# One core, an encoder layer: the list scheduler of the w_o stage gets a landing time for each kind of transfer, and three first evictions go through ScalarE

## The chip, the cores and the metric

The kernel runs on one core of a Trainium2 chip. The metric is the device time of one execution in microseconds; the time of a kernel is the median of its runs. The profile is one more execution of the same program, with its own time.

## The reference, cut to what matters

The reference is one layer of an encoder over 1024 tokens of 1024 channels, in float32. Two branches (a gated mixing of positions and a windowed attention) are merged with sigmoid gates; the merged tensor is multiplied by `w_o`, scaled by a per-channel gate and added to the input; the sum is normalised and goes through a feed-forward network (FFN). The change lies in the middle line of these:

```
merged = jax.nn.sigmoid(gate_a) * a_out + jax.nn.sigmoid(gate_b) * b_out
x = x + gt1 * (merged @ w_o)

h2 = rmsnorm(x, norm2_g) * (1.0 + sc2) + sh2
f_gate, f_up = jnp.split(h2 @ w_ffn_in, 2, axis=-1)
x = x + gt2 * ((jax.nn.silu(f_gate) * f_up) @ w_ffn_out)
```

## The kernel before, in words

Channels lie on the partitions and tokens along the free axis, so the 1024x1024 activations are eight tiles of 128 channels for each half of 512 tokens. A float32 product is made from three passes over operands that are split into a high part (a cast, on ScalarE) and a low part (source minus high part, on VectorE). The large products use a scheme with seven block products in place of eight. Most instructions are issued through one helper, so nearly all rows of the profile have the line L145 (in the changed file L143) and are told apart by their tiles.

`out_products` is the stage of `w_o`. It works on four pairs p0 to p3 of output tiles, and for each pair it makes seven block products, named in the table `USE`: M1, M2, T2, T3, T4, T1 and B22. A product is 12 matmuls of 128x512 (4 blocks by 3 passes). TensorE runs them in three lists: `first` holds the eight products M1 and M2, `second` the twelve T2, T3, T4, and `third` the eight T1, B22. For a pair, M1, T2, T3 and T4 accumulate in the same PSUM bank ("a", tile `mm`). After each of them VectorE reads the bank (an eviction: bank times a gate column, added to a row tile), and the next product of that pair may write the bank only after this eviction has read it. M2 goes to a bank of its own ("b", tile `at`), T1 and B22 share bank "c".

The operands: the token blocks are sums of parts of `merged`, split into high and low tiles. `T1` is tile `tt1h/tt1l`, `T2` is `tt2h/tt2l`, `B22` is `b22h/b22l`; `T3` and `T4` are plain `mid` tiles, made in `blocks` by `negsum` (a SCALAR_TENSOR_TENSOR mid<-mid,mid), a cast and a subtraction (TENSOR_TENSOR mid<-mid,mid). The weights come as units of 1024 columns, loaded into the tile `raw` (three buffers), cast to `wh` and completed with `wl` (three buffers each). `need` asks for them: kind "0" and "B" are parts of `w_o`, kinds "A" and "C" are sums that an earlier stage stored in the DRAM tensor `sO`. In what follows A2 is unit "A" of pair 2, and so on. `("f", 0)` and `("f", 1)`, f0 and f1 for short, are the first units of the FFN's gate weights, split into the tiles `first`. Units of kinds A, B and C come by two transfers of 256 KB each, "0" and f by one of 512 KB.

The row tiles: `c11` holds the input rows that M1 and M2 are added to, in tiles called `xs` (p0, p2) and `hs` (p1, p3). Other rows lie in `mid` tiles, which `new_rows` loads over operands that have been used up; the p-th finished row is squared on ScalarE, added to the sum of squares `ss` on VectorE and stored to the DRAM tensor `x1d` from GpSimd's queue. `even_rows` loads stored rows back.

At the end of the stage stands the normalisation. After T1 of p0 TensorE adds up `ss` over the partitions (`col_sums`, at<-ones,ss), VectorE scales the result (`root_ms`, tile `ms`), GpSimd raises it to the power -1/2 (`root`, tile `rcol`), and after T1 of p1 TensorE spreads it over the partitions (`spread_out`, at<-ident,rcol). Then VectorE scales the rows (`norm_scale`, mid<-mid,mod,at) and splits them with ScalarE into `h`, the operand of the FFN.

The order of all this comes from the class `Plan`. Each step is put down with `add`: its engine (V, A, T, D for transfers issued by SyncE, G for GpSimd), a kind of cost, and the names that it reads and writes. `order` gives each step a latest start, counted back from TensorE's products, and then simulates the engines with the tables `COST` and `WAIT`. T and D keep the order in which they were put down; V, A and G may take any step that is ready. The result fixes each engine's queue. `WAIT` is what passes from a step's end until others can use its result; before the change it is one number for each engine, 3.4 for every transfer.

Of the kernel before, what the change touches and what calls it, by code (L numbers as in the profile page):

```python
# [11 lines left out]
AF = mybir.ActivationFunctionType  # L12
ALU = mybir.AluOpType
# [3 lines left out]
P = 128  # L17
D = 1024
S = 1024
KT = D // P  # L20
HALF = 512
# [19 lines left out]
class Plan:  # L41


    COST = {"v512": 0.6, "v1024": 1.14, "p512": 0.66, "a512": 0.52, "a1024": 0.95, "small": 0.2,
            "load": 0.4, "mm": 2.72, "few": 0.45, "pow": 1.5}
    WAIT = {"V": 0.08, "A": 0.08, "T": 0.4, "D": 3.4, "G": 0.1}

    def __init__(self):
        self.ops, self.last, self.users = [], {}, {}
# [1 line left out]
    def add(self, eng, cost, fn, reads=(), writes=()):  # L51
        n = len(self.ops)
        deps = set()
        for r in reads:
            if r in self.last:
                deps.add(self.last[r])
        for w in writes:
            deps.update(self.users.get(w, ()))
            if w in self.last:
                deps.add(self.last[w])  # L60
        for r in reads:
            self.users.setdefault(r, []).append(n)
        for w in writes:
            self.last[w], self.users[w] = n, []
        self.ops.append((eng, self.COST[cost], fn, deps))

    def order(self, free):

        n = len(self.ops)
        late = [1e9] * n  # L70
        t = 0.0
        for i, (eng, cost, _, _) in enumerate(self.ops):
            if eng == "T":
                late[i] = t
                t += cost
        for i in reversed(range(n)):
            eng, cost, _, deps = self.ops[i]
            for j in deps:
                e, c = self.ops[j][:2]
                late[j] = min(late[j], late[i] - c - self.WAIT[e])  # L80
        queues = {e: [i for i in range(n) if self.ops[i][0] == e] for e in "VATDG"}
        now = {e: free.get(e, 0.0) for e in queues}
        done, start = {}, {}
        while len(start) < n:
            best = None
            for e, q in queues.items():
                for i in q[:1] if e in "TD" else q:
                    deps = self.ops[i][3]
                    if all(j in done for j in deps):
                        at = max([now[e]] + [done[j] for j in deps])  # L90
                        key = (max(at, now[e] + 0.3), late[i], i)
                        if best is None or key < best[0]:
# [5 lines left out]
            done[i] = now[e] + self.WAIT[e]  # L98
        return sorted(range(n), key=lambda i: (start[i], i))

    def run(self, free):
# [6 lines left out]
def kernel(  # L108
# [43 lines left out]
    V, A, G, T = (Engine(e) for e in (nc.vector, nc.scalar, nc.gpsimd, nc.tensor))  # L152
# [24 lines left out]
    def tmp(dt=F32):  # L177
        return t2.tile([P, 512], dt, tag="t2", name=nm("t2"))
# [19 lines left out]
    def load(dst, src):  # L198
        ins = nc.sync.dma_start(dst, src)
        if not manual[0]:  # L200
            tc.keep_in_program_order(ins)

    def store(dst, src):
        nc.gpsimd.dma_start(dst, src)
# [105 lines left out]
    x1d = dram.tile([D, S], F32, tag="x1d", name="x1d")  # L310
# [329 lines left out]
    def x_rows(hf, k):  # L640
        return xB[k * P : (k + 1) * P, :] if hf else xA[:, k * HALF : (k + 1) * HALF]
# [847 lines left out]
    def out_products(merged):  # L1489
# [4 lines left out]
        T2 = oblk["T2"] = (fpt("tt2h"), fpt("tt2l"))  # L1494
# [11 lines left out]
        add = plan.add  # L1506
        tiles, units, banks = {}, {}, {}
        KS = range(4)
# [44 lines left out]

        def make(key, parts, to=None):
# [47 lines left out]
            add("T", "mm", go, [w + "h", w + "l"] + [f"{t}{x}{k}" for x in "hl" for k in KS],  # L1602
                ["b" + str(p) if b == "b" else "a" + str(p)])

        def accumulate(get, tn, p, b, sc, d):
            def go():
                t = get()
                V.scalar_tensor_tensor(out=t, in0=banks[p, b], scalar=sc[:, d : d + 1], in1=t,
                                       op0=ALU.mult, op1=ALU.add)
            add("V", "p512", go, [f"{'b' if b == 'b' else 'a'}{p}"], [tn])  # L1610

        sq = {}
        seen = set()
# [1 line left out]
        def square(get, tn, hf, d):  # L1615
            if hf not in seen:
                seen.add(hf)

                def go():
                    sq[hf] = ss_tile()[:, :HALF]  # L1620
                    A.activation(sq[hf], get(), AF.Square)
                add("A", "a512", go, [tn], ["ss"])
            else:
                q = f"t{count['t'] % 4}"
                count["t"] += 1
                key = ("q", hf, d)
# [7 lines left out]
            add("G", "load", lambda: store(x1d[d * P : (d + 1) * P, hf * HALF : (hf + 1) * HALF], get()),  # L1634
                [tn], [f"x1d{hf}{d}"])

        need("0", 2)
        c11 = [stream(("xs", "hs")[p % 2]) for p in range(NPAIR)]
        for p in range(NPAIR):
            add("D", "load", lambda p=p: load(c11[p], x_rows(0, 2 * p)), [], [f"c{p}"])  # L1640
        blocks()
        first = [(0, "M1"), (1, "M1"), (0, "M2"), (2, "M1"), (1, "M2"), (3, "M1"), (2, "M2"), (3, "M2")]
        for n, (p, name) in enumerate(first):
            product(p, name)
            if n == 2:
                need("0", 3)
            elif n in (4, 6, 7):
                need(*{4: ("A", 0), 6: ("A", 1), 7: ("B", 0)}[n])
            accumulate(lambda p=p: c11[p], f"c{p}", p, "a" if name == "M1" else "b", gt, 2 * p)
            if name == "M2":  # L1650
                square(lambda p=p: c11[p], f"c{p}", 0, 2 * p)

        row = lambda hf, d: (x1B if hf else h2m)[d // 4][:, d % 4, :]
        rn = lambda hf, d: f"{'gh'[hf]}{d}"

        def new_rows(hf, q, old):
            def go():
                if hf == 0 and q == 0:
                    h2[0] = [[hid(), hid()], [hid(), hid()]]
                (x1B if hf else h2m).append(midt(F32, 4))  # L1660
            add("D", "load", go, [], [f"{old}{k}" for k in KS] + [f"{'gh'[hf]}{d}" for d in range(4 * q, 4 * q + 4)])
            for d in range(4 * q, 4 * q + 4):
                if hf or d % 2:
                    add("D", "load", lambda d=d: load(row(hf, d), x_rows(hf, d)), [], [rn(hf, d)])

        def even_rows(q):
            for d in (4 * q, 4 * q + 2):
                add("D", "load", lambda d=d: load(row(0, d), x1d[d * P : (d + 1) * P, :HALF]),
                    [f"x1d0{d}"], [rn(0, d)])

        new_rows(1, 0, "x0")
# [9 lines left out]
        for n, (p, name) in enumerate(second):  # L1681
            product(p, name)
            if n == 2:
                need("A", 2)
            elif n == 3:
                need("A", 3)
                new_rows(1, 1, "m1")
            elif n == 5:
                need("B", 2)
                new_rows(0, 1, "x1")  # L1690
            elif n == 7:
                add("D", "load", new_firsts, [], [f"T2{x}{k}" for x in "hl" for k in KS]
                    + [f"f{i}{x}" for x in "hl" for i in range(2)])
# [12 lines left out]
            accumulate(lambda hf=hf, d=d: row(hf, d), rn(hf, d), p, "a", gt if name == "T2" else ngt, d)  # L1706
            if name == "T4":
                square(lambda d=d: row(0, d), rn(0, d), 0, d)

# [610 lines left out]
```

## Time and profile before

| what | value |
|---|---|
| runs | 1222.55, 1221.06, 1222.39 us; median 1222.39 us |
| the profiled execution's own time | 1221.94 us |
| its span, first to last instruction | 1220.2 us |
| busy in the span | TensorE 1211.0, VectorE 928.5, ScalarE 582.4, GpSimd 150.6 us |
| the w_o stage | about 503 to 584 us of the span |

A row of the timeline gives start and duration of an instruction (or of several equal ones, x4), and in brackets the idle time of its engine just before it with what ended it. Durations overlap a little: the next instruction of an engine starts before the shown end of the one before, so the spacing of two starts is what an instruction costs its queue. PE is TensorE, DVE VectorE, ACT ScalarE, POOL GpSimd; SPq is the queue in which SyncE issues transfers.

### The profile page before, as it was taken

To read this page: it belongs to the slowest core of one execution; us is meant where nothing else is said; L and a number is where in the kernel's file an instruction comes from. 1 tells how busy PE (TensorE), PEld (TensorE's weight loads), DVE (VectorE), ACT (ScalarE), POOL (GpSimd) and SP (SyncE) were. 2 spreads that over 40 slices of the span, in tenths; PEclk is the share of its full clock that TensorE was granted. 3 is DMA by queue.
4 is the path that set the end of the run, shared out by engine and by line. 5 is a ranking of instruction groups with operands and counts; after the bars stand their busy time and mean duration, and the time that the engine had idled before them with its cause. 6 is when DMAs were issued, how large, how long until landed. Compare 5 with 4: busy or idle time off the path is not lost.

```text
span 1220.2 us, 15626 instructions
## 1 busy us (share of the span) xinstructions
PE 1211.0 (99%) x5653; PEld 1007.2 (83%) x5653; DVE 928.5 (76%) x1504; ACT 582.4 (48%) x954; POOL 150.6 (12%) x182
## 2 busy tenths in 40 slices
PE   9999999999999999999999999999999999999998
PEld 7888888888888888877888888888888888888887
DVE  8999977789978776897997767675676766765646
ACT  5667865367855443644553333333333334433341
POOL 0024323024322000001100001000000000000001
PEclk9999999999999999999999999999999999999999
DMA  9752169653277233477313446455555449995552
GB/s 363 284 180 99 35 217 358 248 216 134 104 259 240 96 117 103 148 233 266 103 49 122 172 157 223 173 192 187 190 190 199 163 155 372 394 354 190 190 172 104
DMA packets 78096, 236.54 MB, mean 194 GB/s; under 512 B 8898, under 2 KB 9154, under 8 KB 72772
## 3 DMA queue, kind: packets, MB, share of 16 engines
q1 hardware_dynamic: 63028, 163.20, 38.6%
q0 software_dynamic: 14992, 72.36, 15.8%
q8 instruction: 44, 0.72, 0.3%
q14 instruction: 32, 0.26, 0.1%
HBM read 176.28 MB, written 59.24 MB: 193 GB/s over the span
## 4 chain that ended last, share of the span: by engine, by line
PE 93%; DVE 4%; issue 1%; DMA 1%; ACT 1%; POOL 0%; SPq 0%; DVEq 0%; ACTq 0%; POOLq 0%
PE mm L145 47%; PE at L145 46%; DVE mid L145 2%; DMA raw<-in_w_q_dram 1%; DVE wl L145 1%; DMA mid<-in_xA_dram 0%; DVE ss L145 0%; DVE h L145 0%; DVE ws L145 0%; ACT wh L145 0%; DVE t L145 0%; DVE tt1l L145 0%; ACT mid L145 0%; ACT h L145 0%; DVE b22l L145 0%
## 5 line engine op out<-in xcount | busy, mean ns | idle before, releaser
L145 DVE TENSOR_TENSOR wl<-raw,wh 128x1024 fp32r<-128x1024 f32 (+1 forms) x135 | 159.0, 1182 | 61.7 <-ACT wh L145 61.1
L145 ACT CAST wh<-raw 128x1024 fp32r<-128x1024 f32 (+1 forms) x149 | 152.2, 1023 | 112.1 <-PE mm L145 39.9
L145 PE MATMUL mm<-mid,wh 128*128 128x512 f32 x640 | 197.7, 390 | 0.8 <-DVE mid L145 0.8
L145 PEld LDWEIGHTS mm<-mid,wh 128*128 128x128 f32 x640 | 119.8, 188 | 25.8 <-DVE mid L145 1.2
L145 PE MATMUL mm<-wh,h 128*128 128x512 f32 x384 | 124.7, 397 | 0.5 <-ACT h L145 0.5
L145 PE MATMUL mm<-mid,wl 128*128 128x512 f32 x320 | 124.7, 390 | 0.0
L145 PE MATMUL mm<-h,wh 128*128 128x512 f32 x304 | 94.4, 392 | 0.0
L145 PE MATMUL at<-h,wh 128*128 128x512 f32 x304 | 93.9, 390 | 0.0
L145 PEld LDWEIGHTS mm<-wh,h 128*128 128x128 f32 x384 | 70.8, 188 | 14.2 <-ACT h L145 0.9
L145 DVE TENSOR_TENSOR wl<-ws,wh 128x1024 fp32r<-128x1024 f32 (+1 forms) x54 | 60.8, 1125 | 24.2 <-ACT wh L145 24.1
L145 ACT CAST wh<-ws 128x1024 fp32r<-128x1024 f32 (+1 forms) x54 | 52.5, 973 | 42.9 <-DVE ws L145 28.0
L145 PE MATMUL mm<-wl,h 128*128 128x512 f32 x192 | 71.2, 391 | 0.0
L145 PEld LDWEIGHTS mm<-mid,wl 128*128 128x128 f32 x320 | 60.1, 188 | 12.6
L145 PEld LDWEIGHTS at<-h,wh 128*128 128x128 f32 x304 | 56.9, 188 | 11.7
L145 PEld LDWEIGHTS mm<-h,wh 128*128 128x128 f32 x304 | 56.6, 188 | 11.6
L145 ACT ACTIVATE t<-t 128x512 f32<-128x512 f32 x46 | 28.4, 631 | 71.2 <-DVE t L145 71.2
L145 DVE TENSOR_TENSOR ol<-raw,oh 128x1024 fp32r<-128x1024 f32 x30 | 36.6, 1224 | 31.4 <-ACT oh L145 29.8
L145 PE MATMUL mm<-h,wl 128*128 128x512 f32 x152 | 59.4, 391 | 0.0
L145 PE MATMUL at<-h,wl 128*128 128x512 f32 x152 | 59.3, 390 | 0.0
L145 ACT ACTIVATE xs<-xs 128x512 f32<-128x512 f32 x21 | 13.3, 632 | 94.5 <-DVE xs L145 94.5
L145 ACT CAST oh<-raw 128x1024 fp32r<-128x1024 f32 x30 | 31.6, 1053 | 44.8 <-PE at L145 21.5
L145 PE MATMUL at<-wl,wh 128*128 128x512 f32 (+1 forms) x136 | 52.7, 388 | 0.0
(296 smaller groups left out, 2882.0 us busy)
## 6 DMA issues: line engine op xcount, KB each, us to landing
mid<-in_w_ada_dram SPq DMA_DIRECT2D x28, 512.0 KB, 8.3
raw<-in_w_gate_dram SPq DMA_DIRECT2D x28, 512.0 KB, 3.7
tA<-hid POOLq DMA_DIRECT2D x11, 1024.0 KB, 4.4
tB<-hid POOLq DMA_DIRECT2D x11, 1024.0 KB, 5.0
wo<-in_w_out_dram POOLq DMA_DIRECT2D x22, 512.0 KB, 5.9
wS<-wo POOLq DMA_DIRECT2D x11, 1024.0 KB, 5.2
raw<-wS SPq DMA_DIRECT2D x44, 256.0 KB, 3.4
raw<-tB SPq DMA_DIRECT2D x44, 256.0 KB, 5.2
```

Of the source, the lines that this page charges most:

```text
L145: ins = f(*args, **kw)
```

## The change

Two things change, both in the w_o stage.

First, the planner's tables. `WAIT` no longer holds one number for all transfers: a transfer's landing time now goes by its kind ("load" 3.5, "pair" 4.8, "row" 4.6, "store" 4.0, and "none" 0.0 for steps that only hand over a tile), and the costs get the same kinds. The steps of `fetch`, `new_rows`, `even_rows`, `new_firsts` and the stores are put down under these kinds.

Second, `accumulate` gets a flag `through`. For M1 of p1, p2 and p3 the eviction is split: ScalarE copies the bank times the gate into a temporary tile (`tmp`, tile `t`), and VectorE adds that tile to the row in a step of its own, which may stand later. M1 of p0 is evicted by VectorE as before.

```diff
     COST = {"v512": 0.6, "v1024": 1.14, "p512": 0.66, "a512": 0.52, "a1024": 0.95, "small": 0.2,
-            "load": 0.4, "mm": 2.72, "few": 0.45, "pow": 1.5}
-    WAIT = {"V": 0.08, "A": 0.08, "T": 0.4, "D": 3.4, "G": 0.1}
+            "load": 0.4, "pair": 0.8, "row": 0.4, "none": 0.0, "store": 0.6, "mm": 2.72, "few": 0.45, "pow": 1.5}
+    WAIT = {"V": 0.08, "A": 0.08, "T": 0.4, "G": 0.1, "load": 3.5, "pair": 4.8, "row": 4.6, "none": 0.0, "store": 4.0}
...
-        self.ops.append((eng, self.COST[cost], fn, deps))
+        self.ops.append((eng, self.COST[cost], fn, deps, self.WAIT.get(cost, self.WAIT.get(eng))))
...
-            add("D", "load", go, [], [r])
+            add("D", "load" if len(parts) == 1 else "pair", go, [], [r])
...
-        def accumulate(get, tn, p, b, sc, d):
+        def accumulate(get, tn, p, b, sc, d, through=False):
+            bank = f"{'b' if b == 'b' else 'a'}{p}"
+            if through:
+                q = f"t{count['t'] % 4}"
+                count["t"] += 1
+                key = ("e", tn)
+
+                def copy():
+                    tiles[key] = tmp()
+                    A.activation(tiles[key], banks[p, b], AF.Identity, scale=sc[:, d : d + 1])
+
+                def go():
+                    t = get()
+                    V.tensor_tensor(t, tiles[key], t, op=ALU.add)
+                add("A", "a512", copy, [bank], [q])
+                add("V", "v512", go, [q], [tn])
+                return
+
...
+        THROUGH = (('M1', 1), ('M1', 2), ('M1', 3),)
```

The queues of TensorE and of SyncE's transfers keep their order in the whole program; VectorE, ScalarE and GpSimd are reordered within the stage, and ScalarE has three instructions more. Three places on VectorE follow, the queue before first and the changed one second. In the names, `mm_5066` and `mm_5092` are the banks "a" of p0 and p1 in both programs.

The first place is VectorE between the sums for T3 and the first T2 eviction (`mid_5224<-mm_5066,mod` before, `mid_5233<-mm_5066,mod` after). `mid_5054/5055` is T3, `mid_5056/5057` T4; the three `wl` rows are A0, A1 and B0.

```order
L145 SCALAR_TENSOR_TENSOR mid_4303<-mid_4306,mid_4303 128x512 x4
L145 SCALAR_TENSOR_TENSOR mid_4304<-mid_4306,mid_4304 128x512 x4
L145 TENSOR_TENSOR wl_5198<-raw_5087,wh_5197 128x1024
L145 SCALAR_TENSOR_TENSOR xs_5060<-mm_5066,mod,xs_5060 128x512
L145 SCALAR_TENSOR_TENSOR hs_5061<-mm_5092,mod,hs_5061 128x512
L145 TENSOR_TENSOR mid_5055<-mid_4303,mid_5054 128x512
L145 TENSOR_TENSOR wl_5243<-raw_5130,wh_5242 128x1024
L145 TENSOR_TENSOR mid_5055<-mid_4303,mid_5054 128x512 x3
L145 TENSOR_TENSOR wl_5264<-raw_5162,wh_5263 128x1024
L145 TENSOR_TENSOR mid_5057<-mid_4304,mid_5056 128x512
L145 SCALAR_TENSOR_TENSOR mid_5224<-mm_5066,mod,mid_5224 128x512
```

```order
L143 SCALAR_TENSOR_TENSOR mid_4303<-mid_4306,mid_4303 128x512 x4
L143 TENSOR_TENSOR wl_5202<-raw_5087,wh_5201 128x1024
L143 SCALAR_TENSOR_TENSOR mid_4304<-mid_4306,mid_4304 128x512 x4
L143 SCALAR_TENSOR_TENSOR xs_5060<-mm_5066,mod,xs_5060 128x512
L143 TENSOR_TENSOR mid_5055<-mid_4303,mid_5054 128x512 x2
L143 TENSOR_TENSOR wl_5251<-raw_5131,wh_5250 128x1024
L143 TENSOR_TENSOR mid_5055<-mid_4303,mid_5054 128x512 x2
L143 TENSOR_TENSOR wl_5271<-raw_5177,wh_5270 128x1024
L143 TENSOR_TENSOR mid_5057<-mid_4304,mid_5056 128x512
L143 SCALAR_TENSOR_TENSOR mid_5233<-mm_5066,mod,mid_5233 128x512
```

One row is gone from this stretch, the eviction of M1 of p1 into `hs`; the `wl` rows of A0 and A1 have changed places with rows of the same stretch.

The second place is VectorE a little later, at T3's evictions for p0 and p1 (mid<-mm,ngt from the banks mm_5066 and mm_5092) and the `wl` rows of A2 and A3.

```order
L145 SCALAR_TENSOR_TENSOR xs_5062<-mm_5140,mod,xs_5062 128x512
L145 SCALAR_TENSOR_TENSOR hs_5063<-mm_5183,mod,hs_5063 128x512
L145 TENSOR_TENSOR b22l_5053<-mid_4307,b22h_5052 128x512
L145 SCALAR_TENSOR_TENSOR mid_5224<-mm_5066,ngt_5058,mid_5224 128x512
L145 TENSOR_TENSOR b22l_5053<-mid_4307,b22h_5052 128x512 x3
L145 SCALAR_TENSOR_TENSOR mid_5224<-mm_5092,ngt_5058,mid_5224 128x512
L145 TENSOR_TENSOR wl_5333<-raw_5307,wh_5332 128x1024
L145 TENSOR_TENSOR wl_5350<-raw_5311,wh_5349 128x1024
```

```order
L143 TENSOR_TENSOR b22l_5053<-mid_4307,b22h_5052 128x512 x3
L143 SCALAR_TENSOR_TENSOR mid_5233<-mm_5066,ngt_5058,mid_5233 128x512
L143 TENSOR_TENSOR b22l_5053<-mid_4307,b22h_5052 128x512
L143 TENSOR_TENSOR wl_5342<-raw_5282,wh_5341 128x1024
L143 TENSOR_TENSOR hs_5061<-t_988_5128,hs_5061 128x512
L143 SCALAR_TENSOR_TENSOR mid_5233<-mm_5092,ngt_5058,mid_5233 128x512
L143 TENSOR_TENSOR wl_5364<-raw_5298,wh_5363 128x1024
```

The evictions of M1 for p2 and p3 are gone from here (their additions stand some rows on), and T3's eviction for p1 now stands behind A2's `wl` and the addition for p1.

The third place is VectorE at the end of the second list: the last T4 evictions (banks mm_5140 and mm_5183), the sums into `ss`, and `ms`. The `wl` rows are C0, C1 and C2; mm_5523 and mm_5553, mm_5525 and mm_5559 in the changed program, are the banks of T1 of p0 and p1.

```order
L145 TENSOR_TENSOR wl_5486<-raw_5453,wh_5485 128x1024
L145 SCALAR_TENSOR_TENSOR mid_5360<-mm_5140,ngt_5058,mid_5360 128x512
L145 TENSOR_TENSOR first_5445<-raw_5456,first_5444 128x1024
L145 TENSOR_TENSOR ss_5376<-ss_5376,t_1035_5513 128x512
L145 SCALAR_TENSOR_TENSOR mid_5360<-mm_5183,ngt_5058,mid_5360 128x512
L145 TENSOR_TENSOR wl_5521<-raw_5490,wh_5520 128x1024
L145 TENSOR_TENSOR ss_5376<-ss_5376,t_1040_5538 128x512
L145 TENSOR_TENSOR wl_5542<-raw_5509,wh_5541 128x1024
L145 TENSOR_SCALAR ms_5566<-at_5548 128x4
L145 SCALAR_TENSOR_TENSOR mid_5224<-mm_5523,ngt_5058,mid_5224 128x512
L145 SCALAR_TENSOR_TENSOR mid_5224<-mm_5553,ngt_5058,mid_5224 128x512
```

```order
L143 TENSOR_TENSOR first_5448<-raw_5462,first_5447 128x1024
L143 TENSOR_TENSOR wl_5497<-raw_5458,wh_5496 128x1024
L143 SCALAR_TENSOR_TENSOR mid_5347<-mm_5141,ngt_5058,mid_5347 128x512
L143 TENSOR_TENSOR ss_5382<-ss_5382,t_1038_5519 128x512
L143 SCALAR_TENSOR_TENSOR mid_5347<-mm_5187,ngt_5058,mid_5347 128x512
L143 TENSOR_TENSOR wl_5541<-raw_5493,wh_5540 128x1024
L143 TENSOR_TENSOR ss_5382<-ss_5382,t_1043_5544 128x512
L143 SCALAR_TENSOR_TENSOR mid_5233<-mm_5525,ngt_5058,mid_5233 128x512
L143 TENSOR_SCALAR ms_5573<-at_5551 128x4
L143 TENSOR_TENSOR wl_5557<-raw_5516,wh_5556 128x1024
L143 SCALAR_TENSOR_TENSOR mid_5233<-mm_5559,ngt_5058,mid_5233 128x512
```

`ms` has moved ahead of C2's `wl` and behind the first T1 eviction, and f1's low part (`first`) ahead of C0's `wl`. On ScalarE the cast of f1 has likewise moved ahead of the cast of C0; on GpSimd one more store of a row stands ahead of `rcol`.

More of the change, by code (lines that the diff above doesn't have):

```diff
@@ L71, in order @@
         t = 0.0
-        for i, (eng, cost, _, _) in enumerate(self.ops):
+        for i, (eng, cost, *_) in enumerate(self.ops):
             if eng == "T":
@@ L76, in order @@
         for i in reversed(range(n)):
[L77 to L80, printed above, removed]
+            for j in self.ops[i][3]:
+                late[j] = min(late[j], late[i] - self.ops[j][1] - self.ops[j][4])
         queues = {e: [i for i in range(n) if self.ops[i][0] == e] for e in "VATDG"}
@@ L1609, in go @@
                                        op0=ALU.mult, op1=ALU.add)
[L1610 removed]
+            add("V", "p512", go, [bank], [tn])
         sq = {}
@@ L1633, in square @@
                     [q], ["ss"])
-            add("G", "load", lambda: store(x1d[d * P : (d + 1) * P, hf * HALF : (hf + 1) * HALF], get()),
+            add("G", "store", lambda: store(x1d[d * P : (d + 1) * P, hf * HALF : (hf + 1) * HALF], get()),
                 [tn], [f"x1d{hf}{d}"])
@@ L1691, in out_products @@
             elif n == 7:
-                add("D", "load", new_firsts, [], [f"T2{x}{k}" for x in "hl" for k in KS]
+                add("D", "none", new_firsts, [], [f"T2{x}{k}" for x in "hl" for k in KS]
                     + [f"f{i}{x}" for x in "hl" for i in range(2)])
```

13 lines of the change are left out of this document (7 added, 6 removed).

## The prediction

> **What bounds the kernel now.** I read the totals first, then what TensorE waits for, then the timelines of the engines around each wait.
>
> ```profile
> span 1220.2 us, 15626 instructions
> ...
> PE 1211.0 (99%) x5653; PEld 1007.2 (83%) x5653; DVE 928.5 (76%) x1504; ACT 582.4 (48%) x954; POOL 150.6 (12%) x182
> ...
> PE at L145 <- POOL rcol L145: 1.2, 1, 1.2
> PE mm L145 <- DVE mid L145: 0.8, 1, 0.8
> ...
> PE at L145 <- DVE ss L145: 0.3, 1, 0.3
> ...
> ```
>
> TensorE is busy for 99% of the span, and its order doesn't change. So the change can only win back TensorE's waits, or add some. The list of its waits has six entries; two of those left out are far ahead of this stage, the third lies in the FFN. With that one, the four that count are these (TensorE's timeline, with the last matmul ahead of three of them, and from the chain of waits one unbroken product):
>
> ```profile
> 530.02 0.39 PE L145 MATMUL mm<-tt2h,wl 128*128 128x512 f32 x1
> 531.18 0.74 PE L145 MATMUL mm<-mid,wh 128*128 128x512 f32 x2 [0.78 <-DVE mid L145]
> 561.05 0.39 PE L145 MATMUL mm<-tt1h,wl 128*128 128x512 f32 x1
> 561.75 1.05 PE L145 MATMUL at<-ones,ss 128*128 128x1 f32 x8 [0.31 <-DVE ss L145]
> 562.66 0.48 PE L145 MATMUL mm<-tt1h,wh 128*128 128x512 f32 x1
> 565.28 0.39 PE L145 MATMUL mm<-tt1h,wl 128*128 128x512 f32 x1
> 566.84 1.16 PE L145 MATMUL at<-ident,rcol 128*128 128x128 f32 x8 [1.17 <-POOL rcol L145]
> 616.66 3.00 PE L145 MATMUL at<-h,first 128*128 128x512 f32 x12 [0.31 <-DVE mid L145]
> 647.07 2.72 PE mm L145 x12
> ```
>
> Unbroken, a product of 12 matmuls takes 2.72 us, so a matmul starts 0.23 after the one before. By starts, T3 of p0 comes 531.18 - 530.25 = 0.93 late, the sum over `ss` 561.75 - 561.28 = 0.47, the spreading of `rcol` 566.84 - 565.51 = 1.33. That is 2.73 us, 0.22% of the time: a ceiling for the gain in the stage. The fourth wait lies in the FFN, on a queue of VectorE that starts at the normalisation.
>
> **T3 of p0: one eviction less on the way.** T3 writes the bank that T2's eviction must have read. VectorE before it:
>
> ```profile
> 522.65 1.22 DVE L145 TENSOR_TENSOR wl<-raw,wh 128x1024 fp32r<-128x1024 f32 x1
> 523.79 0.74 DVE L145 SCALAR_TENSOR_TENSOR xs<-mm,mod,xs 128x512 f32<-128x512 f32 x1
> 524.45 0.74 DVE L145 SCALAR_TENSOR_TENSOR hs<-mm,mod,hs 128x512 f32<-128x512 f32 x1
> 525.11 0.68 DVE L145 TENSOR_TENSOR mid<-mid,mid 128x512 fp32r<-128x512 f32 x1
> 525.71 1.22 DVE L145 TENSOR_TENSOR wl<-raw,wh 128x1024 fp32r<-128x1024 f32 x1
> 526.84 1.89 DVE L145 TENSOR_TENSOR mid<-mid,mid 128x512 fp32r<-128x512 f32 x3
> 530.38 0.75 DVE L145 SCALAR_TENSOR_TENSOR mid<-mm,mod,mid 128x512 f32<-128x512 f32 x1
> 519.08 1.05 ACT L145 CAST wh<-raw 128x1024 fp32r<-128x1024 f32 x1
> 535.94 1.05 ACT L145 CAST wh<-raw 128x1024 fp32r<-128x1024 f32 x1 [10.27 <-DMA raw<-sO]
> ```
>
> The queue is dense from 522.65 to 530.38, and the change takes out the `hs` eviction, 525.11 - 524.45 = 0.66 us; the rest is the same work in another order. A0's cast at 519.08 allows its `wl` to go ahead of T4's sums. T2's eviction then starts at 529.72, and T3 at 531.18 - 0.66 = 530.52. I take 0.65 for this; a delay of ScalarE's casts could eat all of it (0), and the ceiling is 0.93.
>
> **What ScalarE adds.** Three ACTIVATEs mm to t with a scale column. No such row exists; the nearest are these: a copy-like read of a bank, and a 128x512 ACTIVATE with a column.
>
> ```profile
> 504.80 0.58 ACT L145 ACTIVATE t<-mm 128x512 f32<-128x512 f32 x1
> 571.71 0.72 ACT L145 ACTIVATE h<-mid,mod 128x512 fp32r<-128x512 f32 x1
> ```
>
> So 3 x 0.58 to 0.72, 1.7 to 2.2 us; I take 0.65 each, nearer to neither. They stand ahead of casts for T2, T3 and T4 whose sums VectorE has yet to make, and ScalarE has 10.27 us idle before 535.94, so I cost them at nothing. Without that cover each would push A1's and B0's casts, and with them T2's eviction, by 0.65.
>
> **What VectorE is spared.** An eviction costs its queue 0.66. The addition that replaces it is a tensor_tensor on tiles of that size: 526.84 to 528.65 for three is 0.60 each. VectorE's total falls by 3 x 0.06 = 0.18 us. The Trainium skill ("VectorE: DVE Perf Modes", Rules for kernel authors) advises to work on a matmul's output where it lies, or to copy it to SBUF first only if many operations follow; here one follows, which speaks against this change. The trace agrees in that the work hardly shrinks, 0.06 of 0.66, and by that alone the gain would be 0.18 us. By the queue above it is the place of the 0.66 that counts, not the amount. I go by the queue and keep the other as a rival.
>
> **T4 of p1: a new wait.** T3's eviction of p1 now stands behind A2's `wl` and an addition, and T4 of p1 needs it. A2's data set the pace there:
>
> ```profile
> 528.80 1.02 SPq L199 DMA_DIRECT2D mid<-in_xA_dram  x2
> 529.87 1.85 SPq L199 DMA_DIRECT2D raw<-sO  x4
> 536.09 1.89 DVE L145 TENSOR_TENSOR b22l<-mid,b22h 128x512 fp32r<-128x512 f32 x3
> 537.89 0.75 DVE L145 SCALAR_TENSOR_TENSOR mid<-mm,ngt,mid 128x512 f32<-128x512 f32 x1
> ```
>
> A2's transfers (529.87) stand on SyncE behind row loads that go off when T3's last low part is done (526.84 + 1.89 = 528.73, and 528.80). That part ends 0.66 sooner, so I let A2 land 0.65 sooner: cast at 535.3, `wl` at 536.35 to 537.5, addition to 538.1, eviction shown until 538.85. TensorE reaches T4 of p1 at 530.52 + 3 x 2.72 = 538.68. A wait of 0.2. If A2 lands no sooner, it is 0.8; if TensorE is held up as much before it, 0.
>
> **The sum over `ss`.** It hangs on f1, whose cast now stands on ScalarE ahead of C0's:
>
> ```profile
> 541.48 0.75 DVE L145 SCALAR_TENSOR_TENSOR hs<-at,mod,hs 128x512 f32<-128x512 f32 x1
> raw<-in_w_gate_dram SPq DMA_DIRECT2D x1, 512.0 KB, 6.3
> 553.49 1.06 ACT L145 CAST first<-raw 128x1024 fp32r<-128x1024 f32 x1 [0.89 <-DMA raw<-in_w_gate_dram]
> ```
>
> f1's load (6.3 us) stands on SyncE behind rows that are read back from `x1d`, and these follow the store of the row that is finished at 541.48. In the new order that eviction starts after T3's eviction (538.1 to 538.75), A3's `wl` (1.14), one eviction (0.66) and one addition (0.60), at 541.1: 0.4 sooner, so f1 lands at about 553.1 (bounds 552.8 and 553.5). From there: cast of f1 0.96, cast of C0 1.05, f1's low part 1.14 and C0's 1.14 on VectorE (the first beside C0's cast, so 0.1 of it shows), T4's eviction of p2 0.75, its square 0.65, addition 0.60, T4's eviction of p3 0.66, C1's `wl` 1.14, the last addition 0.7. C1's cast I take as done by then. That is 7.75, with handovers 8.0, so the sum starts at 561.1 in place of 561.75, **0.65 sooner**. So the 0.2 above costs nothing further: it is passed on VectorE. TensorE reaches this point at 538.9 + 8 x 2.72 = 560.65 and waits 0.45 as before.
>
> **`rcol`: the wait goes.** VectorE and GpSimd before it:
>
> ```profile
> 563.29 1.05 ACT L145 CAST wh<-raw 128x1024 fp32r<-128x1024 f32 x1 [2.92 <-DMA raw<-sO]
> 564.37 1.22 DVE L145 TENSOR_TENSOR wl<-raw,wh 128x1024 fp32r<-128x1024 f32 x1 [2.67 <-ACT wh L145]
> 565.51 0.15 DVE L145 TENSOR_SCALAR ms<-at 128x4 f32<-128x4 f32 x1
> 565.75 1.04 POOL L145 TENSOR_TENSOR rcol<-ms,nhalf 128x4 f32<-128x4 f32 x1 [5.41 <-DVE ms L145]
> 568.04 2.72 DVE L145 SCALAR_TENSOR_TENSOR mid<-mid,mod,at 128x512 f32<-128x512 f32 x4 [1.05 <-PE at L145]
> 559.80 0.54 POOL L204 DMA_DIRECT2D x1d<-mid  x1 [2.17 <-DVE mid L145]
> ```
>
> `ms` needs only the sum at 561.75 to 562.8, but stood behind C2's `wl`, which waited for C2's landing. In the new order only T1's eviction of p0 is ahead of it: from 560.9 to 561.65, so `ms` follows the sum at 562.1, GpSimd issues one store (0.54) inside that time, and `rcol` is there by 563.4. TensorE ends T1 of p1 at 561.1 + 0.91 + 2.85 = 564.86 (durations from 561.75, 562.66 and 565.51) and spreads at once: 564.9 against 566.84, **1.95 sooner in all**. Cover left: 1.4 us. C2's `wl` is now behind `ms`, ahead of the normalisation; at an unchanged landing it ends at 565.5, T1's eviction at 566.2, while the spread result is there at 564.9 + 1.2 = 566.1. So VectorE's queue into the FFN starts 1.85 to 1.95 sooner, and the 0.31 at 616.66 stays. I take **1.9**.
>
> The profiled execution took 1221.94 us, 1.74 more than its span; 1221.94 - 1.9 = 1220.0. It lies 0.45 under the median of the runs, so the forecast for the median is 1222.39 - 1.9 = **1220.5**.
>
> **Rivals.** *The work is only moved* (0.10): T2's eviction is held by ScalarE, whose copies push A1's and B0's casts back by the 0.65 won, and the normalisation by C2, whose `wl` VectorE waits for as before. Then only the spared 0.18 of VectorE's work counts: 1222.2. This is what the rule of the Trainium skill cited above amounts to here. For it speaks that VectorE is dense from 522.65 to 530.38; against it, ScalarE's 10.27 us of idle time and VectorE's 2.67.
>
> *Part is given back* (0.22): C2's buffer comes free with C0's `wl`, which now has f1's 1.14 ahead of it. If C2 lands 1.14 later, its `wl` ends at 566.65, T1's eviction at 567.3, and the normalisation starts 0.75 sooner, not 1.9: 1221.6. This is what its two transfers took:
>
> ```profile
> raw<-sO SPq DMA_DIRECT2D x2, 256.0 KB, 7.0
> raw<-in_w_q_dram SPq DMA_DIRECT2D x7, 512.0 KB, 9.4
> ```
>
> Against it: 7.0 us for 256 KB, where the four of A2 and A3 are issued within 1.85, means a queue, and behind a queue a later issue needn't land later.
>
> *Slower* (0.10): the cast of f1 now has C0's behind it. If f1's load takes 9.4, as the second row shows for its size, f1 lands 3.1 later, at 556.2, the sum over `ss` starts at 564.2 and the spread at 568.0, 1.1 later than before: 1223.5. It decides from a landing at 555.1. Against it: that row's loads are of another stage, and the one here took 6.3.
>
> **How the numbers follow.** The forecast has 0.58, its own range 1219.7 (the ceiling of 2.73) to 1221.0. For the scatter of the runs (1221.06 to 1222.55) I add half a microsecond below; above, the range takes in the first two rivals: 1219.2 to 1222.6, which leaves out the third and the luckiest runs. A difference of 0.2%, 2.44 us, is about what a measurement of this kernel can tell from none; 1.9 lies under it. Faster by more needs a gain near the ceiling or a lucky median: 0.22. Slower by more needs f1 at 557.5 or later, the far part of the third rival: 0.06. The rest, 0.72, is the same.
>
> **What would show it.** Right: no wait on `rcol`; T3 of p0 waits under 0.2; a wait on VectorE of about 0.2 at T4 of p1; 0.3 on `ss` as before; `ms` before C2's `wl`; the spread about 1.9 sooner; waits in the FFN unchanged. Wrong: f1's cast later than 553.5, the normalisation held by C2, or a wait on VectorE at the second sum over `ss` or in the FFN that takes the gain back.

## The result and the profile after

The changed kernel takes 1219.61 us in the median of 22 runs, the kernel before 1221.99 beside it: ratio 0.9982, interval 0.9975 to 0.9988. That is 2.2 us less by the ratio, 2.4 by the medians. The forecast was 1220.5 and a gain of 1.9. It started from the median of three runs, 1222.39, which lies 0.4 above that of the 22; that is 0.4 of the 0.9 us between forecast and median.

The profile after: totals, and the whole list of what TensorE waits for (in all, times, longest).

```profile
span 1217.9 us, 15629 instructions
...
PE 1209.7 (99%) x5653; PEld 1006.8 (83%) x5653; DVE 928.5 (76%) x1504; ACT 584.9 (48%) x957; POOL 150.6 (12%) x182
...
PE at L143 <- DVE identr L143: 1.9, 1, 1.9
PE mm L143 <- ACT h L143: 0.7, 2, 0.6
PE at L143 <- DVE mid L143: 0.3, 1, 0.3
PE at L143 <- DVE ss L143: 0.3, 1, 0.3
PE mm L143 <- DVE xs L143: 0.2, 1, 0.2
```

The waits on `rcol` (1.2) and on `mid` at T3 of p0 (0.8) are gone. Of this list only the 0.2 on `xs` lies in the stage, and it is new; `identr`, `h` and `ss` are waits before 500 us, `mid` is the one in the FFN. VectorE's busy time is the same 928.5; ScalarE has 2.5 us and three instructions more. TensorE's timeline at the places that the prediction speaks of:

```profile
525.13 0.47 PE L143 MATMUL mm<-tt2h,wh 128*128 128x512 f32 x1 [0.25 <-DVE xs L143]
530.45 0.39 PE L143 MATMUL mm<-tt2h,wl 128*128 128x512 f32 x1
530.98 0.73 PE L143 MATMUL mm<-mid,wh 128*128 128x512 f32 x2
560.80 0.39 PE L143 MATMUL mm<-tt1h,wl 128*128 128x512 f32 x1
561.29 1.05 PE L143 MATMUL at<-ones,ss 128*128 128x1 f32 x8
564.82 0.39 PE L143 MATMUL mm<-tt1h,wl 128*128 128x512 f32 x1
565.05 1.05 PE L143 MATMUL at<-ident,rcol 128*128 128x128 f32 x8
```

T3 of p0 starts 0.30 late by starts (0.93 before), the sum over `ss` 0.26 (0.47 before), the spreading of `rcol` not at all (1.33 before). The first row is T2 of p0, which waits for the `xs` eviction. The queues behind these places, VectorE first, then ScalarE with one of the three copies, GpSimd and SyncE:

```profile
530.17 0.76 DVE L143 SCALAR_TENSOR_TENSOR mid<-mm,mod,mid 128x512 f32<-128x512 f32 x1
536.35 1.24 DVE L143 TENSOR_TENSOR wl<-raw,wh 128x1024 fp32r<-128x1024 f32 x1
537.49 0.70 DVE L143 TENSOR_TENSOR hs<-t,hs 128x512 f32<-128x512 f32 x1
538.09 0.76 DVE L143 SCALAR_TENSOR_TENSOR mid<-mm,ngt,mid 128x512 f32<-128x512 f32 x1
557.54 0.69 DVE L143 TENSOR_TENSOR ss<-ss,t 128x512 f32<-128x512 f32 x1 [0.76 <-ACT t L143]
558.51 0.75 DVE L143 SCALAR_TENSOR_TENSOR mid<-mm,ngt,mid 128x512 f32<-128x512 f32 x1 [0.28 <-PE mm L143]
559.40 1.23 DVE L143 TENSOR_TENSOR wl<-raw,wh 128x1024 fp32r<-128x1024 f32 x1
560.55 0.68 DVE L143 TENSOR_TENSOR ss<-ss,t 128x512 f32<-128x512 f32 x1
562.38 0.16 DVE L143 TENSOR_SCALAR ms<-at 128x4 f32<-128x4 f32 x1 [0.40 <-PE at L143]
563.64 1.23 DVE L143 TENSOR_TENSOR wl<-raw,wh 128x1024 fp32r<-128x1024 f32 x1 [1.10 <-ACT wh L143]
510.55 0.68 ACT L143 ACTIVATE t<-mm,mod 128x512 f32<-128x512 f32 x1
511.13 1.13 ACT L143 CAST b22h<-mid 128x512 fp32r<-128x512 f32 x2
552.67 1.05 ACT L143 CAST first<-raw 128x1024 fp32r<-128x1024 f32 x1 [2.26 <-DMA raw<-in_w_gate_dram]
558.32 1.05 ACT L143 CAST wh<-raw 128x1024 fp32r<-128x1024 f32 x1 [0.82 <-PE mm L143]
562.83 1.04 POOL L143 TENSOR_TENSOR rcol<-ms,nhalf 128x4 f32<-128x4 f32 x1
524.39 0.81 SPq L197 DMA_DIRECT2D mid<-in_xA_dram  x2
525.30 2.85 SPq L197 DMA_DIRECT2D raw<-sO  x4
536.48 0.80 SPq L197 DMA_DIRECT2D mid<-in_xA_dram  x2
```

`ms` (562.38) follows the sum and no longer C2's `wl` (563.64), as forecast. What the forecast did not have stands in the other rows. Between f1's low part (553.76) and the sum over `ss`, VectorE is idle twice: 0.76 for a square on ScalarE, which belongs to the chain that starts at f1, and 0.28 for TensorE, which does not. So in this execution f1 does not set the sum. And C1's cast (558.32), put down to TensorE, starts 0.1 us after C1's second half landed (558.22; a landing is that of a unit's last transfer, as the trace records it). The sum starts 2.97 behind that cast, and in the kernel before too: 561.75 behind this row of its timeline, which is C1's cast, 0.1 after a landing at 558.68.

```profile
558.78 1.05 ACT L145 CAST wh<-raw 128x1024 fp32r<-128x1024 f32 x1 [1.26 <-PE mm L145]
```

So three theories. **Forecast**: VectorE's order decides; the copies are worth 0.65 (T3 of p0), `ms`'s place 1.3, and f1's landing sets the sum. **V**: VectorE's order alone decides, f1 sets the sum and `ms` the spreading. **L**: the landings of C1 and C2 decide, which go off in one burst from SyncE. (The expectations of the first four kernels were written before L was formed. Their theory A is the forecast with its two terms apart, B says that sooner landings bring the gain, C that another wait eats it.)

### The profile page after: what moved, and what is told of

Read it like the earlier page. It is cut to its first block, busy times and chain, and to the rows that moved or that the text cites. A ratio compares the mean times of both kernels' runs of the same rounds, so it can differ in the third digit from the quotient of the medians.

```text
span 1217.9 us, 15629 instructions
## 1 busy us (share of the span) xinstructions
PE 1209.7 (99%) x5653; PEld 1006.8 (83%) x5653; DVE 928.5 (76%) x1504; ACT 584.9 (48%) x957; POOL 150.6 (12%) x182
## 4 chain that ended last, share of the span: by engine, by line
PE 90%; DVE 5%; DMA 3%; issue 1%; ACT 1%; SPq 0%; DVEq 0%; ACTq 0%
PE at L143 46%; PE mm L143 45%; DVE mid L143 2%; DMA mid<-in_w_ada_dram 1%; DVE wl L143 1%; DMA raw<-in_w_q_dram 1%; DMA raw<-in_w_ada_dram 1%; DVE ss L143 0%; DVE t L143 0%; DMA mid<-in_xA_dram 0%; DMA raw<-sO 0%; ACT wh L143 0%; DVE raw L143 0%; DVE h L143 0%; DVE ws L143 0%
```

## The experiments

**Each half of the change alone, and each forecast term alone.** The new tables without copies (`tables_only`), and the copies with the old numbers (`copies_only`):

```diff
-        THROUGH = (('M1', 1), ('M1', 2), ('M1', 3),)
+        THROUGH = ()
```
```diff
-            "load": 0.4, "pair": 0.8, "row": 0.4, "none": 0.0, "store": 0.6, ...
-    WAIT = {..., "load": 3.5, "pair": 4.8, "row": 4.6, "none": 0.0, "store": 4.0}
+            "load": 0.4, "pair": 0.4, "row": 0.4, "none": 0.4, "store": 0.4, ...
+    WAIT = {..., "load": 3.4, "pair": 3.4, "row": 3.4, "none": 3.4, "store": 0.1}
```

In the kernel before, C2's `wl` put behind `ms` (`ms_first`; the plan's steps 176 and 183, T1's evictions stay behind both), and M1 of p1 alone copied on ScalarE and added behind T3's eviction of p1 (`one_copy`):

```diff
+        seq = self.order(free)
+        for i, j in ((176, 183),):
+            seq.remove(i)
+            seq.insert(seq.index(j) + 1, i)
```
```diff
+            if (p, b, tn) == (1, "a", "c1"):
+                def copy():
+                    tiles["e"] = tmp()
+                    A.activation(tiles["e"], banks[p, b], AF.Identity, scale=sc[:, d : d + 1])
+                plan.extra = (copy, lambda: V.tensor_tensor(get(), tiles["e"], get(), op=ALU.add))
+                add("V", "p512", None, ["a1"], [tn])
+                return
...
+            if n == place:
+                self.extra[0]()
+            if i == 126:
+                self.extra[1]()
```

> The new tables without the copies (no M1 goes through ScalarE). VectorE's order then has ms ahead of C2's wl as in the change, and all four M1 evictions as before it. Theory A (two separate terms: 0.65 us from the eviction taken out ahead of T3 of p0, 1.3 us from ms no longer standing behind C2's wl): 1.3 us faster than before, no wait on rcol, T3 of p0 still waits 0.8. Rival B (the gain comes from earlier landings, above all the row loads that go out 4.4 us sooner): the whole gain of about 2 us if those loads go out sooner here too, else none.

> The copies with the old tables. VectorE has no hs eviction ahead of T3 of p0, but ms stands behind C2's wl as before the change. Theory A: 0.65 us faster, T3 of p0 waits 0.2 or less, rcol still waits 1.2. Rival C (the terms don't add up alone: what the copies win is spent waiting for C2's landing, which sets ms): 0 to 0.3 us faster, with the wait on rcol grown to 1.5 to 1.9. Rival B: 0.

> The kernel before with one step moved by hand: C2's wl goes behind ms on VectorE, all else in its old order. Theory A: 1.3 us faster, no wait on rcol, the other waits as before (0.8 on T3 of p0, 0.3 on ss). If C2's wl then holds the normalisation instead, 0.7 to 1.0. Rival B: no difference.

> The kernel before with one step moved by hand: M1 of p1 is copied on ScalarE after the first B22 cast, and VectorE adds it behind T3's eviction of p1; all else in its old order. Theory A: T3 of p0 waits 0.2 or less in place of 0.8, and the time falls by 0.65 us. Rival C: T3 of p0 waits less, but rcol waits the more (up to 1.8) and the time falls by 0 to 0.3 us. If C2's loads go out sooner too, because SyncE's queue waits for TensorE ahead of them, A's number.

Measured, with the kernel before at 1222.08: tables alone 1225.13, ratio 1.0016 (1.0006 to 1.0027), slower. Copies alone 1219.85, 0.9977 (0.9967 to 0.9988), the whole gain. `ms_first` 1221.64, 0.9989 (0.9977 to 1.0): 1.3 us by the ratio, 0.4 by the medians, and an interval that reaches to nothing, so the forecast's 1.3 is neither shown nor excluded. `one_copy` 1222.87, 1.0006 (0.9994 to 1.0018), nothing. So the split of the gain into 0.65 for the copies and 1.3 for the tables is wrong: the two don't add.

TensorE's starts tell where each part goes. T2 of p0 to T3 of p0 takes 6.50 us before, 5.85 after, 5.85 with one copy, 5.91 with the tables, 6.39 with the copies alone. What counts is the amount of work on VectorE between the `xs` eviction and T2's: the changed kernel and one copy have lost the `hs` eviction there; the copies alone have lost it too, but a subtraction for T4 (0.60) came in; the tables alone keep `hs` (523.94), but such a subtraction went out. With one copy the 0.65 is lost further on (TensorE's timeline):

```profile
563.12 1.05 PE L151 MATMUL at<-ones,ss 128*128 128x1 f32 x8 [2.12 <-DVE ss L151]
564.39 0.63 PE L151 MATMUL mm<-tt1l,wh 128*128 128x512 f32 x1
564.82 0.63 PE L151 MATMUL mm<-tt1h,wl 128*128 128x512 f32 x1
```

The sum comes 2.96 behind C1's cast here too, but C1 landed at 560.06, 1.4 later than before, though SyncE issued it 0.4 sooner (553.08 and 553.52). Its landings are late from C0 on (553.18, before 551.44). After the wait a matmul starts every 0.43 us, not 0.23. With the copies alone SyncE's queue is another: C1 and C2 stand ahead of the first load of `w_up` (tile `ws`), where the other kernels of this group have that load first.

```profile
551.76 0.80 SPq L197 DMA_DIRECT2D raw<-sO  x2
555.33 0.43 SPq L1258 DMA_DIRECT2D ws<-in_w_up_dram  x1
```

C1 landed at 555.56, C2 at 560.33, and the wait on `rcol` is gone although `ms` still stands behind C2's `wl`. This speaks for L. It also means that this kernel does not show what the copies are worth: the moved load alone will turn out to gain as much (`before_ws_late`, below), and no run has the three copies with the old tables and the old queue of SyncE.

With the tables alone f1 landed as late as in the forecast's slower rival (ScalarE, VectorE and SyncE):

```profile
556.23 1.05 ACT L143 CAST first<-raw 128x1024 fp32r<-128x1024 f32 x1 [6.50 <-DMA raw<-in_w_gate_dram]
557.19 1.04 ACT L143 CAST wh<-raw 128x1024 fp32r<-128x1024 f32 x1
557.32 1.23 DVE L143 TENSOR_TENSOR first<-raw,first 128x1024 fp32r<-128x1024 f32 x1 [4.40 <-ACT first L143]
539.11 1.28 DVE L143 TENSOR_TENSOR b22l<-mid,b22h 128x512 fp32r<-128x512 f32 x2
540.42 0.80 SPq L197 DMA_DIRECT2D mid<-in_xA_dram  x2
547.22 1.38 SPq L197 DMA_DIRECT2D mid<-x1d  x2
```

B22's last low parts end at 540.4, behind evictions that the copies would have taken out; with the whole change the same loads of rows go off at 536.48. Here they wait until 540.42, run beside the stores to `x1d`, the rows are read back at 547.22 in place of 543.54, and f1 lands at 556.21 with C0's cast, whose data came at 554.95, behind it. The rival had put that landing down to a long transfer, 9.4 us; here it took 6.5 and was issued late, at 549.74 in place of 546.19.

**The landings.** The kernel before profiled again (`control`), and the kernel before with one transfer moved and no other instruction (`before_ws_late`): the 512 KB load of the first block of `w_up`, which stands ahead of C1's halves and waits for TensorE's T3 of p3, goes behind C3's. (The next load of `w_up`, tile `ru`, also comes behind one more load of gate weights.)

```diff
         ins = nc.sync.dma_start(dst, src)
+        issued.append(ins)
...
-            dma(RU[f], w_up[f])
+            ins = nc.sync.dma_start(RU[f], w_up[f])
+            if f == 0:
+                after(ins, issued[-6])
```

> The kernel before, unchanged, profiled once more. It gives the scatter of single landings and waits. Theory L (the landings of C1's and C2's halves set the end of the stage; they come in one burst that SyncE starts after TensorE's T3 of p3) expects f1 within 0.7 us of 553.46, C1 of 558.68 and C2 of 563.19, the sum over ss 2.9 to 3.1 us behind the cast of C1, and a wait of 0.8 to 1.6 us on rcol. If single landings scatter by more than 1 us, comparisons of single profiles below that size mean nothing here, and only the medians count. The time: 1221 to 1223.

> The kernel before with one DMA moved and no compute instruction: the 512 KB load of the first w_up block, which stands on SyncE ahead of C1's halves and waits there 5.6 us for TensorE (T3 of p3), is put behind C3's halves. Theory L: C1 goes off when f0's low part has freed its buffer, 552.3 instead of 553.5, and without 512 KB (about 1.3 us at 400 GB/s) ahead of it, so it lands about 2 us sooner (556.7); C2 lands about 1.2 us sooner (562.0), its low part, ms and rcol as much, so that the wait on rcol falls from 1.2 to about 0.2, the spread starts 1.2 us sooner: 1220.8, ratio 0.999. The sum over ss gains 0.2 to 0.3 of this. Theory V (VectorE's order alone decides: f1 sets the sum, ms the spread): f1's load is ahead of the moved one, nothing moves: 1222.1, rcol's wait stays 1.2. Beyond both: the moved load comes too late for the first w_up parts and the FFN waits: 1223.

Measured: `control` 1221.87 in its one run. Its landings differ from the first profile by -0.4 (f1), +0.7 (C1) and +0.3 (C2), its waits on `ss` and `rcol` are 1.0 and 0.7, and the sum again comes 2.97 behind C1's cast. `before_ws_late` 1220.32, ratio 0.998 (0.9972 to 0.9988): one load moved on SyncE gains as much as the whole change. SyncE and TensorE of it:

```profile
552.77 0.80 SPq L200 DMA_DIRECT2D raw<-sO  x2
561.56 1.05 PE L145 MATMUL at<-ones,ss 128*128 128x1 f32 x8
565.28 1.05 PE L145 MATMUL at<-ident,rcol 128*128 128x128 f32 x8
```

C1 landed at 556.92 and C2 at 561.39, both 1.8 sooner than before; the spreading moved 1.6, and the wait on `rcol` is gone with VectorE's order untouched. The sum moved only 0.2, because TensorE itself came to it 0.26 later; it is no longer late (0.02, before 0.47). V expected nothing here and falls. L holds for the end of the stage.

**The place of `ms`, and of the last addition.** In the changed kernel, `ms` (and the power) put back behind C2's `wl` (`ms_behind`, measured twice, the second time beside the changed kernel); and the last square ahead of C1's cast with the last addition into `ss` ahead of C1's `wl` (`sum_first`).

```diff
+        for i, j in ((186, 179), (187, 186)):              # ms_behind
+        for i, j in ((182, 181), (166, 182), (167, 166)):  # sum_first
+            seq.remove(i)
+            seq.insert(seq.index(j) + 1, i)
```

> The changed kernel with ms (and the power on GpSimd after it) put back behind C2's low part on VectorE, all else as changed. Theory: C2 lands at 562.45 there, cast to 563.6, low part to 564.8, ms 564.9, rcol by 566.1; the spread starts at 566.1 to 566.3 instead of 565.05, so 1.1 us slower than the changed kernel, 1220.7, with a wait on rcol of about 1.1. Rival: the sooner landing of C2 alone takes the wait away, as where only the copies were made: 1219.7, no wait on rcol.

> The changed kernel with the last square on ScalarE put ahead of C1's cast, and the last addition into ss on VectorE ahead of C1's low part. Theory L (the sum over ss waits for C1's landing, which has its cast and low part ahead of the last addition): the addition follows T4's last eviction (to 559.2) and the square (559.8) at once and ends by 560.5, so the sum starts at 560.8 when TensorE comes to it, no wait on ss (0.45 before, 0.3 as shown), and C1's low part (to 561.7) is still there when T1 of p1 needs it at 562.1: 0.4 us faster than the changed kernel, 1219.2. Theory V (f1's landing and the work behind it set the sum): the wait stays 0.2 to 0.3 and the time 1219.6. Against both: C1's low part is now late for T1 of p1, TensorE waits for wl there, and nothing is won.

> The changed kernel, unchanged, run beside the other three on one chip and profiled once more. 1219.6, ratio 0.998; the scatter of landings as in the kernel before: f1, C1 and C2 within 1 us of 552.65, 558.22 and 562.45, and the sum over ss 2.9 to 3.1 us behind the cast of C1.

> The changed kernel with ms behind C2's low part, once more, now beside the changed kernel on one chip. From C2's landing to the spread there are cast 1.05, low part 1.14, ms 0.15, handovers and the power 1.04, together 3.7 us; TensorE comes to the spread at 564.8 to 565.0, so a wait shows only where C2 lands after 561.2. It landed at 561.09 in the first look and at 562.45 in the changed kernel. Theory: the landing scatters over both sides, so the place of ms is worth 0.3 to 0.9 us in the median: 1220.1 to 1220.5 where the changed kernel has 1219.6. Rival: C2 nearly always lands in time once VectorE's queue has moved up, and ms's place is worth nothing: both within 0.2 us of each other. My forecast's term (1.3 us for the wait on rcol) would need the full 1.1 to 1.3.

Measured: the changed kernel again 1219.89, 0.9973 (0.9963 to 0.9983); `ms_behind` 1220.52, 0.9983 (0.9974 to 0.9992), and 1220.72, 0.9979 (0.997 to 0.9989), beside it. So `ms`'s place is worth about 0.8 us in the changed kernel, with intervals that overlap. In its two profiles C2 landed at 561.09 and 561.94, and the spreading came 0.2 and 0.3 later behind the sum than in the changed kernel (3.95 and 4.07, where that has 3.76). That the price follows C2's landing fits, but two profiles do not show all of the 0.8.

These profiles show one thing more. Here the sum comes 3.2 and 3.3 behind C1's cast, not 2.97, and 8.03 behind f1's landing in both (552.77 and 560.80, 553.49 and 561.52), with VectorE busy or waiting for the square all the way; with the tables alone it was 8.03 too (556.21 and 564.24). ScalarE and TensorE of the second:

```profile
553.51 1.05 ACT L147 CAST first<-raw 128x1024 fp32r<-128x1024 f32 x1 [2.87 <-DMA raw<-in_w_gate_dram]
561.52 1.05 PE L147 MATMUL at<-ones,ss 128*128 128x1 f32 x8
```

The forecast's chain from f1 was 8.0. So in the changed order the sum comes at the later of two chains, 8.0 behind f1's landing and 2.97 behind C1's cast, and not before TensorE gets there.

`sum_first` 1219.95, 0.9976 (0.9967 to 0.9984), no faster than the changed kernel. The sum was freed of C1 as L expects (C1 landed at 559.17, the sum started 2.06 behind that, where the changed kernel has 3.07), but the time went into a wait on `rcol`. VectorE and GpSimd of it:

```profile
563.12 0.15 DVE L147 TENSOR_SCALAR ms<-at 128x4 f32<-128x4 f32 x1
563.50 0.54 POOL L206 DMA_DIRECT2D x1d<-mid  x1 [3.05 <-DVE ms L147]
564.05 1.93 POOL L147 TENSOR_TENSOR rcol<-ms,nhalf 128x4 f32<-128x4 f32 x1
```

and in the list of TensorE's waits:

```profile
PE at L147 <- POOL rcol L147: 0.9, 1, 0.9
```

The store that stands ahead of the power now goes off later than `ms`, and the power itself took 1.93 in place of 1.04.

**f1 ahead of C0, and both edits together.** The tables alone with f1's cast and low part put back behind C0's (`tables_f1_back`); the changed kernel with the load of `w_up` moved as above (`after_ws_late`).

```diff
+        for i, j in ((160, 155), (161, 169)):              # tables_f1_back
+            seq.remove(i)
+            seq.insert(seq.index(j) + 1, i)
```

> The new tables without copies, with f1's cast and low part put back behind C0's. With the tables alone f1 landed at 556.21 and C0's cast and low part, though landed at 554.95, stood behind it; TensorE then waited 1.4 us at T1 of p0, 1.9 on ss, and ran at half its rate for 3.4 us. Theory F (the late f1 ahead of C0 did it): C0's cast goes at 555.0, its low part ends by 557.3 when T1 of p0 needs it, the sum over ss starts 2.97 behind C1's cast (559.2), at 562.2 instead of 564.2, with a wait of about 1 us and no stretch at half rate, the spread at 566.0 to 566.5: 1221.5 to 1222, ratio 1.000 or below, against 1225.1 and 1.0016. Theory R (the rows that SyncE issues late, behind B22's last low parts, delay C0 and C1 themselves): the wait on ss stays near 2 us and the time at 1224 or more.

> The changed kernel with the first w_up load put behind C3's halves on SyncE, which is the edit that alone made the kernel before 2 us faster. Theory L: C1 lands about 1.5 us sooner than in the changed kernel (556.7), C2 1.2 sooner (561.2); the sum over ss is then held by T4's last eviction, square and addition alone and starts 0.1 to 0.3 sooner, and the spread as much: 1219.3, 0.3 faster than the changed kernel, and its slow tail (runs above 1221.5) is gone. If instead both edits took away the same waits and nothing else stands there, the two are alike within 0.2. If the sum of both gains came (2 and 2), 1217.6: excluded by the waits of 0.3 that are left.

Measured: `tables_f1_back` 1221.16, 0.9988 (0.9979 to 0.9997), against 1.0016 with f1 in front, though f1 landed as late (556.54) and the rows were read back as late (547.80). So what made the tables alone slow is the late f1 ahead of C0, and not C0's or C1's own landings (555.31 and 559.19, with the tables alone 554.95 and 559.13). The sum starts at 562.56 in place of 564.24, and two stops of 0.72 each at T1 of p0 are gone. The wait on `ss` is still 2.1, where 1 was expected, since TensorE without those stops comes to the sum 1.9 sooner. `after_ws_late` 1219.87, 0.9972 (0.9961 to 0.9982): the same as the changed kernel beside it (1219.89). The two edits take away the same waits and don't add. No kernel beat the change by more than the intervals allow.

## Why the prediction was right, step by step

| stretch of TensorE, us | before, twice | forecast | after, twice |
|---|---|---|---|
| T2 of p0 to T3 of p0 | 6.50, 6.51 | -0.65 | 5.85, 5.85 |
| T3 of p0 to the sum over `ss` | 30.57, 31.27 | 0 | 30.31, 31.04 |
| the sum to the spreading of `rcol` | 5.09, 4.67 | -1.33 | 3.76, 3.76 |

**T3 of p0** was right in place and size: one eviction less in a dense queue, 0.65 of 0.65. T2's eviction itself started at 530.17, not 529.72, since T2 began 0.45 later in that execution. T2's start, which follows the `xs` eviction by 0.89 or 0.90 us in all four profiles, is outside this stretch: it came 0.13 and 0.16 late before, 0.40 and 0.13 after, so in the first profile 0.27 of the 0.65 was spent there. The forecast had no such term. `before_ws_late`, with VectorE's old order, has 0.47, so it is scatter and not the copies.

**ScalarE's copies** are spaced 0.58 (510.55 to 511.13), the lower bound, where 0.65 was taken. They cost TensorE nothing that shows.

**The work that VectorE is spared** was a false rival: its busy time did not change (928.5), the eviction and the addition are spaced 0.66 and 0.60, and the gain came all the same. The Trainium skill's advice ("VectorE: DVE Perf Modes", Rules for kernel authors) against a copy for one use agrees with the amount of work in this trace, but it was the place of the work that told: the same copies with one subtraction more in that stretch shorten it by 0.11 only.

**T4 of p1** did not wait; 0.2 was forecast. The step that failed is that A2's data set the pace. A2 was issued at 525.30, not 529.87: the row loads ahead of it now go off behind T4's sums (524.39, where the sums end at 521.83 + 2.49), and no longer behind T3's last low part. A2's `wl` starts at 536.35, exactly as forecast, but because VectorE's queue is dense up to there; its landing never counted, and that the number fits is luck, in an execution that ran 0.45 late at T2.

**The sum over `ss`** is the step that was wrong in its reason. 0.65 sooner was forecast from f1's landing; 0.46 was measured in one profile and 0.93 in the other, and each equals what C1's landing moved: 558.68 before, 558.22 and 557.75 after. The chain from f1 was sized rightly, 8.0: from f1's landings (552.65 and 552.58) it would have been done at 560.7 and 560.6, 0.6 and 0.2 ahead of the sum (561.29 and 560.82). It was not the last to end, since C1's `wl` stands ahead of the last addition. The forecast took C1's cast "as done by then", without looking up when C1 lands; that its 0.65 lies between the two measured gains is luck.

**`rcol`**: the wait is gone and the stretch is 3.76, the forecast's 0.91 + 2.85. Of the cover of 1.4 us 1.2 was there (the power ends at 562.83 + 1.04, the spreading starts at 565.05). The normalisation starts at 566.14, 1.90 sooner, as forecast. The price of the old order is not a fixed 1.3: it is 1.33 and 0.91 in the two profiles of before, and 0.2 to 0.3 or nothing where C2 lands sooner.

**The rivals.** "Part is given back" did not happen: C2's halves were issued at 555.23 (555.42 before) and landed 0.7 sooner. "Slower" did not happen in the changed kernel, where f1 landed at 552.65, but its price is real: with the tables alone f1 landed at 556.21, where the forecast priced the sum at 564.2 (measured 564.24) and the spreading at 568.0 (measured 569.59; the rest is the clock, below). Its cause was another, a late issue and not a long transfer. With the new tables the copies keep f1 in time, by clearing VectorE ahead of B22's low parts: this is the coupling that the forecast missed.

What stays open: why C1 landed 1.4 later with one copy though it was issued sooner. C0 and f1 were late as well (1.7 and 1.4), and the kernel before has 0.7 of scatter in C1 alone. Its 12 runs gained nothing either, which fits, but they have no trace, and no run shows which transfer held C1 up. Open too is what the three copies are worth with the old tables, since that kernel had another queue on SyncE.

## To carry to other kernels

Ask of each wait which landing stands ahead of it, and what SyncE issued just before that transfer: one 512 KB load in front of two halves was worth as much as a replanned stage. List every chain that ends at a wait with its own end time, and not only the one that looks longest. A wait that the profile puts down to a matmul or to a cast may be a landing 0.1 us earlier. And gains of two edits that shorten paths to the same wait don't add, while one edit can hold the cover that the other needs, so test the halves before splitting a gain between them, and see that a half leaves every queue as it was, SyncE's too.

## What was not expected of the hardware

After a wait TensorE may run at half its rate. The same window (start and end, length, PE busy with its count, granted clock, DMA share, GB/s) of the tables alone:

```profile
564.00:568.00 4.00, 3.76 (x14) 0.61 0.93 272
```

of one copy:

```profile
564.00:568.00 4.00, 4.00 (x13) 0.57 0.82 279
```

and of the tables with f1 put back:

```profile
564.00:568.00 4.00, 4.00 (x23) 1.00 0.95 301
```

In the first two, the matmuls after the wait on `ss` (1.94 us with two stops of 0.72 shortly before, and 2.12 us) are spaced 0.43 us for about 3.4 us, then 0.23 again: some 1.7 us lost beyond the wait. In the third the wait was as long (2.12) and the clock stayed. The Trainium skill ("TensorE: Matmul & The Clock Gate", Part 1) has half rate after an idle window of about 3.4 us that runs freely of the kernel, and names about 3.4 us as the limit for gaps. Half rate and length agree with these rows, but here stops of 2.1 us and less were followed by it at times.

Of 91 runs of the kernel before with a clock on record, 32 have a mean clock of 0.998 or less, with a median of 1223.3 against 1222.0 for the others; of the changed kernel's 31 runs, 2. Among the runs at a higher clock the change goes from 1222.0 to 1219.6, 2.4 us, so the gain does not come from the clock alone; the long runs at the lower clock become rare. That they have a stretch such as the one above is not shown: neither profile of the kernel before has one in the stage.
